# A hybrid mLSTM and S5 block on one core: conversions, attention steps and the merge put in another order

## The chip, the cores and the metric

The kernel runs on one core of a Trainium2 chip. The core has a matrix engine (PE), a vector engine (DVE), a scalar engine (ACT), a general engine (POOL) and SyncE (SP), on whose queue this kernel issues its DMA transfers. Each engine works off its own instructions in order and waits on semaphores that the others raise. The metric is the device time of one execution, in microseconds (us).

## The reference

The input is x, 1024 tokens by 1024 channels, in float32. The reference computes, for one layer:

```python
xn = rmsnorm(x, norm_pre_g)
u_a, z_a, o_a, i_a, f_a, u_b, z_b, g_pre = split(xn @ w_in)
y_a = mlstm_branch(u_a, z_a, o_a, i_a, f_a, ...) @ w_a_out
y_b = s5_branch(u_b, z_b, ...) @ w_b_out
g = sigmoid(g_pre)
merged = g[:, :1024] * y_a + g[:, 1024:] * y_b
out = x + rmsnorm(merged @ w_o, norm_post_g)
# mlstm_branch, for each of 4 heads of width 256, in 8 chunks of 128 tokens:
c = silu(causal_conv(u_a, width 4) + conv_b)
q, k, v = c @ w_q, c @ w_k, u_a @ w_v
h = chunkwise gated attention of q, k, v with a 256 x 256 state carried from chunk to chunk
h = rmsnorm(sigmoid(o_a) * h) * head_g + skip * c;  h = h * silu(z_a)
```

## The kernel before

**Precision.** Each float32 operand of a large product is kept as a pair, a high part (names ending in h: wh, xh, hlh, mh) and the rest (wl, xl, hll, ml), and `dot3` issues three matmuls for each step: high x high (L180), then the two mixed ones (L181, L182). A weight comes from DRAM as raw tile wr. `split_w` makes wh on ACT (L140) and wl = wr - wh on DVE (L142), in pieces of at most 128x1024; with `pl=True` the second and later pieces of wl are made by POOL.

**Weights in turn.** `order` lists the weights in the order of their use. `fetch` issues the DMAs of the next raw weight, `pump` converts the raw weight that has come (if none is converted and waiting) and puts off a `fetch`, and `take` hands out the converted one and, unless told not to, pumps the next.

**Units.** The program is written as units, each a group of matmuls into one PSUM bank of 512 float32 with the work on the other engines that empties it. There are three banks named pp for projections and five named pm for attention. `run` and `fill` issue a unit; `fill(n)` takes the next n from the list `fillers`. `defer` puts off a unit's second part to a later unit, and a unit's loads (its `pre`) are issued `look[0]` units ahead.

**Heads.** While head h does its attention, chunk by chunk, the projections of head h+1 fill the gaps: first eight o_units (the output gate, 24 matmuls of 128x256 each), then u and z units. In a chunk, `attn_a(h, c)` forms the scores and the scaled keys ksh and ksl, `attn_b(h, c)` uses them against v; `attn_d(h, hf)` normalises a half (L1170, DVE, tile hr), and transposes it (L1180, PE, 8 transposes). Behind chunk 7 come five `late` units in the order u2, k0, v0, u3, v1. The unit u3 is the `u_unit` with m = 1 and hf = 1: it makes hlh and hll, pumps the next weight, and does a width-4 causal convolution over its bank: a bias on ACT (tile t2k), then on DVE for each of three taps an operation on the bank (L961) and a small one on the columns kept from the half before (L964, halo). In the last head there is no next head; the fillers are units of y_a (`ya_unit`), which multiply six of the eight channel tiles' worth of head outputs by w_a_out's quarters, tile names y_t1 and y_gb, and store partial sums to the DRAM buffer pa_d.

**Merge and output.** `ya_unit(3, ...)` makes the last quarter of y_a's partial sums, `mg_unit(ct, hf)` reads ft and fpa (`mg_pre`'s loads of t1_d and pa_d), adds the remaining channel tiles with the weight called ya3, and writes mh (ACT) and ml (POOL). `wo_unit(i, t)` multiplies the merged rows of row block t (128 tokens) by quarter i of w_o, squares the bank on ACT for the norm (fjk, with the sum in sso) and multiplies it by the norm's weight on DVE (ob). The order of all of this is the order in which the Python code issues it; no scheduler moves it.

Of the kernel before, what the change touches and what calls it, by code (L numbers as in the profile page):

```python
# [10 lines left out]
F32 = mybir.dt.float32  # L11
# [3 lines left out]
ALU = mybir.AluOpType  # L15
# [21 lines left out]
def hybrid_block(ctx, tc, x, norm_pre_g, w_in, conv_w, conv_b, w_q, w_k, w_v, b_i, b_f, head_g,  # L37
# [49 lines left out]
    def defer(f, n=1):  # L87
        stage2.append([n, f])
# [854 lines left out]
    def u_unit(h, m, hf):  # L943
        o = bank()
        proj_cm(o, cur["u"], m * P, xh, xl, HS[hf])
        ct = 2 * h + m
        hi, lo = ht((P, 512), "hlh", 5, F32R), ht((P, 512), "hll", 5, F32R)
        A.activation(hi, o, AF.Copy)
        tt(lo, o, hi.bitcast(F32), ALU.subtract)
        uhl[h, m, hf] = (hi, lo)  # L950
        if m and hf:
            pump(pl=True)
        acc = ht((P, 512), "t2k", 6)
        A.activation(acc, o, AF.Identity, scale=cw[:, 3, ct:ct + 1], bias=cb[:, ct:ct + 1])
        if hf == 0:
            hl_ = ht((P, 4), "halo", 4)
            V.tensor_copy(hl_[:, 0:3], o[:, 509:512])
            halo[h, m] = hl_
        for j in (2, 1, 0):
            s = 3 - j  # L960
            V.scalar_tensor_tensor(acc[:, s:], o[:, :512 - s], cw[:, j, ct:ct + 1], acc[:, s:],  # L961
                                   op0=ALU.mult, op1=ALU.add)
            if hf == 1:
                V.scalar_tensor_tensor(acc[:, :s], halo[h, m][:, 3 - s:3], cw[:, j, ct:ct + 1],  # L964
                                       acc[:, :s], op0=ALU.mult, op1=ALU.add)
        defer(lambda: u_act(h, m, hf, acc), (3 if h < H - 1 else 2) if m and hf else 1)

    def u_act(h, m, hf, acc):
# [246 lines left out]
            SY.dma_start(yh[k][:, HS[hf]].bitcast(F32), yh_d[k * P:(k + 1) * P, HS[hf]])  # L1215
            SY.dma_start(yl[k][:, HS[hf]].bitcast(F32), yl_d[k * P:(k + 1) * P, HS[hf]])

    yaux = {}

    def ya_pre(ct, hf, pool=None):  # L1220
        rs = slice(ct * P, (ct + 1) * P)
        pool, a, b, n = (hp, "hlh", "hll", 5) if pool is None else (pool, "ft", "fpa", 7)
        t1 = pool.tile([P, 512], F32, tag=a, bufs=n, name="y_t1")
        SY.dma_start(t1, t1_d[rs, HS[hf]])
        gb = pool.tile([P, 512], F32, tag=b, bufs=n, name="y_gb")
        SY.dma_start(gb, gb_d[rs, HS[hf]])
        yaux[ct, hf] = (t1, gb)

    def ya_unit(i, m, hf):
        if m == 0 and hf == 0 and i < 3:  # L1230
            cur["ya"] = take(("ya", i), i > 0)
        ct = 2 * i + m
        rs = slice(ct * P, (ct + 1) * P)
        t1, gb = yaux.pop((ct, hf))
        o = bank()
        proj_cm(o, cur["ya"], m * P, yh, yl, HS[hf], ks=list(range(6)))
        V.scalar_tensor_tensor(t1, t1, 1.0, o, op0=ALU.add, op1=ALU.mult)
        V.scalar_tensor_tensor(gb, gb, 0.25, t1, op0=ALU.mult, op1=ALU.add)
# [30 lines left out]
    for h in range(H):  # L1269
        k1 = unit(ks[1])  # L1270
        if h < H - 1:
            us, os_, zs = proj_units(h + 1)
            ks, vs_ = kv_units(h + 1)
            late = [us[2], ks[0], vs_[0], us[3], vs_[1]]
            mix = os_ + [us[0], zs[0], us[1], zs[1], zs[2], zs[3]]
            fillers.extend(unit(f) for f in mix)
            fillers.insert(6, k1)
        else:
            late = []
            for i in range(3):  # L1280
                for hf in range(2):
                    for m in range(2):
                        fillers.append(unit(lambda i=i, m=m, hf=hf: ya_unit(i, m, hf),
                                            lambda ct=2 * i + m, hf=hf: (ct, hf) in yaux or ya_pre(ct, hf)))
            fillers.insert(3, k1)
        look[0] = 2 if h == H - 1 else 1
        load_so(h, 0)
        load_so(h, 1)
        if h == H - 1:
            for i in range(2):  # L1290
                fillers[i][0]()
                fillers[i] = (None,) + fillers[i][1:]
        ystep(4)
        if h < H - 1:
            fill()
        attn_a(h, 0)
        for c in range(NCH):
            if c == 1 or c == 6:
                load_cz(h, c // 4)
            if c == 6 and h == H - 2:  # L1300
                alloc_y(0)
            fill()
            ystep(3)
            if 1 <= c < NCH - 1:
# [12 lines left out]
            if c % 4 != 3 if h < H - 1 else c in (2, 4, 6):
                fill()
        if h == H - 1:
            fill(2)  # L1320
            attn_d(h, 1)
        for i, f in enumerate(late):
            run(unit(f))
            if i == (3 if h < H - 2 else 2):
                attn_d(h, 1)
            if i == 3 and h == H - 2:
                ya_pre(0, 0)
                alloc_y(1)
                ystep(2)
        while fillers:  # L1330
            fill()
        tick()
    cur["ya"] = take(("ya", 3))
    flush2()
    hb_.close()

# [2 lines left out]
    gpo = fp.tile([P, D], F32, name="gpo")  # L1339
    SY.dma_start(gpo, norm_post_g[0].partition_broadcast(P))  # L1340
    mh, ml = {}, {}
    maux = {}

    def mg_pre(ct, hf):
        rs = slice(ct * P, (ct + 1) * P)
        t1 = fp.tile([P, 512], F32, tag="ft", bufs=7, name="ft")
        SY.dma_start(t1, t1_d[rs, HS[hf]])
        pr = fp.tile([P, 512], F32, tag="fpa", bufs=7, name="fpa")
        SY.dma_start(pr, pa_d[rs, HS[hf]])
        maux[ct, hf] = (t1, pr)  # L1350

    def mg_unit(ct, hf):
        if ct == 0 and hf == 0:
            cur["ya3"] = take("ya3", False)
        t1, pr = maux.pop((ct, hf))
        o = bank()
        proj_cm(o, cur["ya3"], ct * P, yh, yl, HS[hf], ks=[6, 7])
        V.scalar_tensor_tensor(t1, t1, 1.0, o, op0=ALU.add, op1=ALU.mult)
# [4 lines left out]
        defer(lambda: PL.tensor_tensor(ml[ct, hf], t1, mh[ct, hf].bitcast(F32), op=ALU.subtract))  # L1363

    ob, xres = {}, {}
    sso = fp.tile([P, NCH, 4], F32, name="sso")

    def wo_unit(i, t):
        if t == 0:
            cur["wo", i] = take(("wo", i), i > 0)  # L1370
        if i == 0:
            ob[t] = main.tile([P, D], F32, tag=f"xh{t}", name=f"ob{t}")
            xres[t] = main.tile([P, D], F32, tag=f"xl{t}", name=f"xr{t}")
        if i == 1:
            SY.dma_start(xres[t], x[0, t * P:(t + 1) * P, :])
# [7 lines left out]
        A.activation(jk, o[:, :256], AF.Square, accum_out=sso[:, t, i:i + 1])
        mul(ob[t][:, cs], o[:, :256], gpo[:, cs])
        if i == 3:
            s = fp.tile([P, 1], F32, tag="fs", bufs=4, name="fs")
            V.tensor_reduce(s, sso[:, t, :], axis=mybir.AxisListType.X, op=ALU.add)
            V.tensor_scalar(s, s, 1.0 / D, 4.0 * EPS, op0=ALU.mult, op1=ALU.add)
            PL.tensor_tensor(s, s, halfm[:, 0:1], op=ALU.pow)
            finish(t, s)  # L1390

# [5 lines left out]
            store(out[0, t * P:(t + 1) * P, qs_], ob[t][:, qs_])  # L1397

    def mgf(ct, hf):
        fillers.append(unit(lambda: mg_unit(ct, hf), lambda: mg_pre(ct, hf)))  # L1400

    def yaf(m, hf):
        fillers.append(unit(lambda: ya_unit(3, m, hf), lambda: ya_pre(6 + m, hf, fp)))

    todo = deque((ct, hf) for hf in range(2) for ct in range(KT))
    for m, hf in ((0, 0), (1, 0), (0, 1), (1, 1)):
        yaf(m, hf)
        mgf(*todo.popleft())
        mgf(*todo.popleft())
    for ct, hf in todo:  # L1410
        mgf(ct, hf)
    look[0] = 3
    for i in range(3):
        fillers[i][0]()
        fillers[i] = (None,) + fillers[i][1:]
    fill(10)
    pump()
    fill(4)
    for t in range(NCH):
        run(unit(lambda: wo_unit(0, t)))  # L1420
        fill(3)
        if t == 1:
            pump()
    for i in range(1, 4):
# [32 lines left out]
```

## Time and profile before

| | |
|---|---|
| median of 3 runs | 1007.21 us (1006.0, 1007.21, 1008.55) |
| profiled execution | 1006.37 us, span 1004.3 us |
| busy PE, DVE, ACT, POOL | 976.7, 615.5, 351.1, 154.6 us |
| DMA | 148.31 MB, mean 148 GB/s |
| chain that ended last | PE 83%, DVE 10%, DMA 3% |

The span is the time from the first to the last instruction that the profiler saw; the execution's own time has some 2 us more. A row of a timeline has the start, the length, the engine, the line, the operation, output <- input, the shape, and in brackets the idle time just before it with what ended that.

### The profile page before, as it was taken

To read this page: it belongs to the slowest core of one execution; us is meant where nothing else is said; L and a number is where in the kernel's file an instruction comes from. 1 tells how busy PE (TensorE), PEld (TensorE's weight loads), DVE (VectorE), ACT (ScalarE), POOL (GpSimd) and SP (SyncE) were. 2 spreads that over 40 slices of the span, in tenths; PEclk is the share of its full clock that TensorE was granted. 3 is DMA by queue.
4 is the path that set the end of the run, shared out by engine and by line. 5 is a ranking of instruction groups with operands and counts; after the bars stand their busy time and mean duration, and the time that the engine had idled before them with its cause. 6 is when DMAs were issued, how large, how long until landed. Compare 5 with 4: busy or idle time off the path is not lost.

```text
span 1004.3 us, 15220 instructions
## 1 busy us (share of the span) xinstructions
PE 976.7 (97%) x5617; PEld 840.9 (84%) x5617; DVE 615.5 (61%) x1400; ACT 351.1 (35%) x696; POOL 154.6 (15%) x210
## 2 busy tenths in 40 slices
PE   7999999999999999999999999999999999999997
PEld 6888888788778788978988899889987888779997
DVE  4426496686952854254677477747774888675226
ACT  7322131233032531223544355435543452223311
POOL 4001000000000000012112232223221311343001
PEclk8999999999999999999999999999999999999999
DMA  7344221333056447314433354336436796783504
GB/s 253 94 153 157 90 95 36 93 111 109 17 177 187 170 156 253 107 42 126 138 121 131 95 174 131 135 86 184 132 121 215 248 318 202 271 301 118 189 1 168
DMA packets 115449, 148.31 MB, mean 148 GB/s; under 512 B 19080, under 2 KB 71472, under 8 KB 115376
## 3 DMA queue, kind: packets, MB, share of 16 engines
q1 hardware_dynamic: 115376, 147.35, 45.7%
q8 instruction: 44, 0.72, 0.3%
q14 instruction: 29, 0.24, 0.1%
HBM read 100.88 MB, written 46.43 MB: 147 GB/s over the span
## 4 chain that ended last, share of the span: by engine, by line
PE 83%; DVE 10%; DMA 3%; issue 2%; ACT 1%; SPq 0%; POOL 0%; DVEq 0%; POOLq 0%; ACTq 0%
PE pp L180 22%; PE pp L182 22%; PE pp L181 22%; PE pm L182 4%; PE pm L180 4%; PE pm L181 3%; DVE wl L142 1%; PE pm L1084 1%; DMA wr<-in_w_in_dram 1%; DVE zt L439 1%; PE pm L1007 1%; DMA xt<-in_x_dram 1%; DMA ft<-t_d 1%; PE pm L661 1%; DVE ec_r L439 1%
## 5 line engine op out<-in xcount | busy, mean ns | idle before, releaser
L180 PE MATMUL pp<-xh,wh 128*128 128x512 f32 x768 | 307.6, 401 | 3.2 <-DVE xl L276 2.4
L182 PE MATMUL pp<-xh,wl 128*128 128x512 f32 x768 | 305.0, 397 | 4.4 <-DVE wl L142 4.4
L181 PE MATMUL pp<-xl,wh 128*128 128x512 f32 x768 | 304.7, 397 | 0.0
L182 PEld LDWEIGHTS pp<-xh,wl 128*128 128x128 f32 x768 | 145.0, 189 | 41.0 <-DVE wl L142 6.2
L180 PEld LDWEIGHTS pp<-xh,wh 128*128 128x128 f32 x768 | 145.0, 189 | 39.3 <-DVE xl L276 2.7
L181 PEld LDWEIGHTS pp<-xl,wh 128*128 128x128 f32 x768 | 145.1, 189 | 32.7
L142 DVE TENSOR_TENSOR wl<-wr,wh 128x1024 fp32r<-128x1024 f32 (+2 forms) x71 | 83.4, 1211 | 46.3 <-ACT wh L140 41.7
L140 ACT ACTIVATE wh<-wr 128x1024 fp32r<-128x1024 f32 (+2 forms) x76 | 73.2, 1008 | 40.8 <-PE pm L181 30.7
L182 PE MATMUL pp<-wh,ml 128*128 128x256 f32 x256 | 72.8, 284 | 0.5 <-POOL ml L1363 0.5
L180 PE MATMUL pp<-wh,mh 128*128 128x256 f32 x256 | 72.9, 285 | 0.0
L180 PE MATMUL pp<-wh,xh 128*128 128x256 f32 (+1 forms) x256 | 72.0, 281 | 0.0
L181 PE MATMUL pp<-wl,mh 128*128 128x256 f32 x256 | 71.9, 281 | 0.0
L288 ACT ACTIVATE tg<-pp 128x512 f32<-128x512 f32 x32 | 19.1, 599 | 151.1 <-PE pp L182 75.2
L181 PE MATMUL pp<-wl,xh 128*128 128x256 f32 (+1 forms) x256 | 71.8, 280 | 0.0
L182 PE MATMUL pp<-wh,xl 128*128 128x256 f32 (+1 forms) x256 | 71.8, 280 | 0.0
L182 PEld LDWEIGHTS pp<-wh,ml 128*128 128x128 f32 x256 | 48.1, 188 | 0.7 <-POOL ml L1363 0.7
L181 PEld LDWEIGHTS pp<-wl,mh 128*128 128x128 f32 x256 | 48.6, 190 | 0.1
L180 PEld LDWEIGHTS pp<-wh,mh 128*128 128x128 f32 x256 | 48.4, 189 | 0.2 <-ACT mh L1362 0.2
L181 PEld LDWEIGHTS pp<-wl,xh 128*128 128x128 f32 x256 | 48.2, 188 | 0.2
L180 PEld LDWEIGHTS pp<-wh,xh 128*128 128x128 f32 x256 | 48.1, 188 | 0.2
L182 PEld LDWEIGHTS pp<-wh,xl 128*128 128x128 f32 x256 | 48.0, 187 | 0.0
L981 POOL TENSOR_TENSOR hll<-t2k,hlh 128x512 fp32r<-128x512 f32 x16 | 20.8, 1297 | 166.2 <-ACT hlh L980 89.4
(395 smaller groups left out, 1731.5 us busy)
## 6 DMA issues: line engine op xcount, KB each, us to landing
wr<-in_w_in_dram SPq DMA_DIRECT2D x48, 512.0 KB
t_d<-tg SPq DMA_DIRECT2D x32, 256.0 KB
xt<-in_x_dram SPq DMA_DIRECT2D x8, 512.0 KB
aux<-t_d SPq DMA_DIRECT2D x16, 256.0 KB
gb_d<-aux SPq DMA_DIRECT2D x16, 256.0 KB
so_d<-sow SPq DMA_DIRECT2D x32, 128.0 KB
sz_d<-t2k SPq DMA_DIRECT2D x16, 256.0 KB
cs_d<-t2k SPq DMA_DIRECT2D x16, 256.0 KB
```

The costliest lines, as they stand in the source:

```text
L140: A.activation(hi, raw, AF.Copy)
L142: eng.tensor_tensor(wl[:, k0:k0 + n, c0:c0 + w], raw, hi.bitcast(F32), op=ALU.subtract)
L180: PE.matmul(o, lh, rh, start=first, stop=False)
L181: PE.matmul(o, lh, rl, start=False, stop=False)
L182: PE.matmul(o, ll, rh, start=False, stop=last)
L288: A.activation(t, o, AF.Tanh, scale=0.5)
L439: V.tensor_tensor(o, a, b, op=op)
L661: PE.matmul(o[NS * b2:NS * (b2 + 1), g * P:(g + 1) * P], q["wt"][:, ri, g, NS * b2:NS * (b2 + 1)], ut[b][:, 2 * g + b2, :], start=True, st ...
L981: PL.tensor_tensor(lo, acc, hi.bitcast(F32), op=ALU.subtract)
L1007: PE.matmul(pm[:, 256 * k:256 * k + 256], wt[:, e, 256 + P * k:256 + P * k + P], wt[:, e, 0:256], start=e == 0, stop=e == 1)
L1084: PE.matmul(sc[:, :P], k_[:, m, sl], q_[:, m, sl], start=m == 0, stop=m == 1)
```

## The change

In words, part by part:

- `u_unit`: the pump stands behind the convolution instead of ahead of it.
- The heads' loop: two fillers between attn_a(h, 0) and attn_b(h, 0) instead of one, and one more or less at two other chunks to keep the count; attn_d of the second-last head stands behind u3, as in the other heads; two of the four deferred y loads of the last head's entry come later.
- Before the merge: the last quarter of w_a_out is taken without a pump, and ya3 is pumped with `pl=True`.
- `ya_unit(3, ...)`: its four results stay on chip (tiles fyt, fyg, fyp), so that for channel tiles 6 and 7 the stores to pa_d and the loads in `mg_pre` are left out; ft and fpa have 4 buffers instead of 7.
- The merge's list: ya(0,0), ya(1,0), mg(6,0), mg(7,0), mg(0,0), ya(0,1), mg(1,0), ya(1,1), and then the rest, instead of one ya and two mg in turn. With fill(6) and then fill(2) for each row block (before: 4 and 3) the pump at t = 1 stands ahead of the last two merge units (ct = 4, 5 of the second half).
- `wo_unit`: the norm's sum over the first three quarters is formed with the third; the mean's factor is in the square's scale; the last addition is POOL's.

```diff
         tt(lo, o, hi.bitcast(F32), ALU.subtract)
         uhl[h, m, hf] = (hi, lo)
-        if m and hf:
-            pump(pl=True)
         acc = ht((P, 512), "t2k", 6)
         A.activation(acc, o, AF.Identity, scale=cw[:, 3, ct:ct + 1], bias=cb[:, ct:ct + 1])
...
                 V.scalar_tensor_tensor(acc[:, :s], halo[h, m][:, 3 - s:3], cw[:, j, ct:ct + 1],
                                        acc[:, :s], op0=ALU.mult, op1=ALU.add)
+        if m and hf:
+            pump(pl=True)
         defer(lambda: u_act(h, m, hf, acc), (3 if h < H - 1 else 2) if m and hf else 1)
 
...
             SY.dma_start(yl[k][:, HS[hf]].bitcast(F32), yl_d[k * P:(k + 1) * P, HS[hf]])
 
-    yaux = {}
+    yaux, maux = {}, {}
 
     def ya_pre(ct, hf, pool=None):
         rs = slice(ct * P, (ct + 1) * P)
-        pool, a, b, n = (hp, "hlh", "hll", 5) if pool is None else (pool, "ft", "fpa", 7)
+        pool, a, b, n = (hp, "hlh", "hll", 5) if pool is None else (pool, "fyt", "fyg", 2)
         t1 = pool.tile([P, 512], F32, tag=a, bufs=n, name="y_t1")
         SY.dma_start(t1, t1_d[rs, HS[hf]])
...
         o = bank()
         proj_cm(o, cur["ya"], m * P, yh, yl, HS[hf], ks=list(range(6)))
-        V.scalar_tensor_tensor(t1, t1, 1.0, o, op0=ALU.add, op1=ALU.mult)
+        t1_ = t1
+        if i == 3:
+            t1 = fp.tile([P, 512], F32, tag="fyp", bufs=2, name="fyp")
+        V.scalar_tensor_tensor(t1, t1_, 1.0, o, op0=ALU.add, op1=ALU.mult)
         V.scalar_tensor_tensor(gb, gb, 0.25, t1, op0=ALU.mult, op1=ALU.add)
-        store(pa_d[rs, HS[hf]], gb)
+        if i < 3:
+            store(pa_d[rs, HS[hf]], gb)
+        else:
+            maux[ct, hf] = (t1_, gb)
 
     def proj_units(h):
...
                 fillers[i][0]()
                 fillers[i] = (None,) + fillers[i][1:]
-        ystep(4)
+        ystep(4 if h < H - 1 else 2)
         if h < H - 1:
             fill()
...
             if c == 6 and h == H - 2:
                 alloc_y(0)
-            fill()
+            fill(2 if c == 0 and h < H - 1 else 1)
             ystep(3)
             if 1 <= c < NCH - 1:
...
             if c == 1:
                 decay(h, 1)
-            if c % 4 != 3 if h < H - 1 else c in (2, 4, 6):
+            if c in (1, 2, 4, 5, 6) if h < H - 1 else c in (2, 4, 6):
                 fill()
         if h == H - 1:
...
         for i, f in enumerate(late):
             run(unit(f))
-            if i == (3 if h < H - 2 else 2):
+            if i == 3:
                 attn_d(h, 1)
             if i == 3 and h == H - 2:
...
             fill()
         tick()
-    cur["ya"] = take(("ya", 3))
+    cur["ya"] = take(("ya", 3), False)
+    pump(pl=True)
     flush2()
     hb_.close()
...
     SY.dma_start(gpo, norm_post_g[0].partition_broadcast(P))
     mh, ml = {}, {}
-    maux = {}
 
     def mg_pre(ct, hf):
         rs = slice(ct * P, (ct + 1) * P)
-        t1 = fp.tile([P, 512], F32, tag="ft", bufs=7, name="ft")
+        t1 = fp.tile([P, 512], F32, tag="ft", bufs=4, name="ft")
         SY.dma_start(t1, t1_d[rs, HS[hf]])
-        pr = fp.tile([P, 512], F32, tag="fpa", bufs=7, name="fpa")
+        pr = fp.tile([P, 512], F32, tag="fpa", bufs=4, name="fpa")
         SY.dma_start(pr, pa_d[rs, HS[hf]])
         maux[ct, hf] = (t1, pr)
 
     def mg_unit(ct, hf):
-        if ct == 0 and hf == 0:
+        if "ya3" not in cur:
             cur["ya3"] = take("ya3", False)
         t1, pr = maux.pop((ct, hf))
...
 
     ob, xres = {}, {}
-    sso = fp.tile([P, NCH, 4], F32, name="sso")
+    sso = fp.tile([P, NCH, 5], F32, name="sso")
 
     def wo_unit(i, t):
...
         cs = slice(256 * i, 256 * (i + 1))
         jk = fp.tile([P, 256], F32, tag="fjk", bufs=2, name="fjk")
-        A.activation(jk, o[:, :256], AF.Square, accum_out=sso[:, t, i:i + 1])
+        A.activation(jk, o[:, :256], AF.Square, scale=1.0 / 32.0, accum_out=sso[:, t, i:i + 1])
         mul(ob[t][:, cs], o[:, :256], gpo[:, cs])
+        if i == 2:
+            V.tensor_reduce(sso[:, t, 4:5], sso[:, t, 0:3], axis=mybir.AxisListType.X, op=ALU.add)
+            V.tensor_scalar(sso[:, t, 4:5], sso[:, t, 4:5], 4.0 * EPS, None, op0=ALU.add)
         if i == 3:
             s = fp.tile([P, 1], F32, tag="fs", bufs=4, name="fs")
-            V.tensor_reduce(s, sso[:, t, :], axis=mybir.AxisListType.X, op=ALU.add)
-            V.tensor_scalar(s, s, 1.0 / D, 4.0 * EPS, op0=ALU.mult, op1=ALU.add)
+            PL.tensor_tensor(s, sso[:, t, 3:4], sso[:, t, 4:5], op=ALU.add)
             PL.tensor_tensor(s, s, halfm[:, 0:1], op=ALU.pow)
             finish(t, s)
...
 
     def mgf(ct, hf):
-        fillers.append(unit(lambda: mg_unit(ct, hf), lambda: mg_pre(ct, hf)))
+        fillers.append(unit(lambda: mg_unit(ct, hf), lambda: (ct, hf) in maux or ct > 5 or mg_pre(ct, hf)))
 
     def yaf(m, hf):
         fillers.append(unit(lambda: ya_unit(3, m, hf), lambda: ya_pre(6 + m, hf, fp)))
 
-    todo = deque((ct, hf) for hf in range(2) for ct in range(KT))
-    for m, hf in ((0, 0), (1, 0), (0, 1), (1, 1)):
-        yaf(m, hf)
-        mgf(*todo.popleft())
-        mgf(*todo.popleft())
-    for ct, hf in todo:
+    yaf(0, 0)
+    yaf(1, 0)
+    mgf(6, 0)
+    mgf(7, 0)
+    mgf(0, 0)
+    yaf(0, 1)
+    mgf(1, 0)
+    yaf(1, 1)
+    n_ya = len(fillers)
+    for ct, hf in [(ct, 0) for ct in range(2, 6)] + [(6, 1), (7, 1)] + [(ct, 1) for ct in range(6)]:
         mgf(ct, hf)
     look[0] = 3
...
         fillers[i][0]()
         fillers[i] = (None,) + fillers[i][1:]
-    fill(10)
+    fill(n_ya)
     pump()
-    fill(4)
+    fill(6)
     for t in range(NCH):
         run(unit(lambda: wo_unit(0, t)))
-        fill(3)
+        fill(2)
         if t == 1:
             pump()
...
```

What the change moves, at three places. In the lists a name's number tells which tile of that name it is. First DVE at u3 of head 1, which is issued behind the attention of head 0; pp_5213 is u3's bank, wl_5243 (before) and wl_5251 (after) the next weight, which the first o_unit among the fillers of the next head reads. Before:

```order
L439 TENSOR_TENSOR hll_5239<-pp_5213,hlh_5238 128x512
L142 TENSOR_TENSOR wl_5243<-wr_5100,wh_5242 128x1024
L961 SCALAR_TENSOR_TENSOR t2k_5248<-pp_5213,par_147,t2k_5248 128x511
L964 SCALAR_TENSOR_TENSOR t2k_5248<-halo_4890,par_147,t2k_5248 128x1
L961 SCALAR_TENSOR_TENSOR t2k_5248<-pp_5213,par_147,t2k_5248 128x510
L964 SCALAR_TENSOR_TENSOR t2k_5248<-halo_4890,par_147,t2k_5248 128x2
L961 SCALAR_TENSOR_TENSOR t2k_5248<-pp_5213,par_147,t2k_5248 128x509
L964 SCALAR_TENSOR_TENSOR t2k_5248<-halo_4890,par_147,t2k_5248 128x3
L1182 SCALAR_TENSOR_TENSOR t2k_5261<-pm_5256,par_147,cz_4902 128x512
```

After:

```order
L439 TENSOR_TENSOR hll_5239<-pp_5213,hlh_5238 128x512
L959 SCALAR_TENSOR_TENSOR t2k_5242<-pp_5213,par_147,t2k_5242 128x511
L962 SCALAR_TENSOR_TENSOR t2k_5242<-halo_4890,par_147,t2k_5242 128x1
L959 SCALAR_TENSOR_TENSOR t2k_5242<-pp_5213,par_147,t2k_5242 128x510
L962 SCALAR_TENSOR_TENSOR t2k_5242<-halo_4890,par_147,t2k_5242 128x2
L959 SCALAR_TENSOR_TENSOR t2k_5242<-pp_5213,par_147,t2k_5242 128x509
L962 SCALAR_TENSOR_TENSOR t2k_5242<-halo_4890,par_147,t2k_5242 128x3
L142 TENSOR_TENSOR wl_5251<-wr_5100,wh_5250 128x1024
L1182 SCALAR_TENSOR_TENSOR t2k_5261<-pm_5256,par_147,cz_4902 128x512
```

The conversion moved behind all six operations of the convolution; ACT's bias and its two wh changed places in the same way.

Second SP's queue at the merge, around the raw weights of w_o's second quarter, wr. Before:

```order
L1347 DMA ft_8793<-t1_d_68 128x512
L1349 DMA fpa_8795<-pa_d_81 128x512
L82 DMA pa_d_81<-y_gb_8735 128x512
L124 DMA wr_8826<-in_w_o_dram 128x4x256
L124 DMA wr_8828<-in_w_o_dram 128x4x256
L1347 DMA ft_8830<-t1_d_68 128x512
L1349 DMA fpa_8832<-pa_d_81 128x512
L1347 DMA ft_8846<-t1_d_68 128x512
```

After:

```order
L1353 DMA ft_8751<-t1_d_68 128x512
L1355 DMA fpa_8753<-pa_d_81 128x512
L124 DMA wr_8784<-in_w_o_dram 128x4x256
L124 DMA wr_8786<-in_w_o_dram 128x4x256
L1353 DMA ft_8788<-t1_d_68 128x512
L1355 DMA fpa_8790<-pa_d_81 128x512
```

Before, three loads for channel tiles 2, 3 and 4 and the last store of y_a stand ahead of wr. After, ft_8788 and fpa_8790, of channel tile 5, the last merge unit ahead of the second half's tiles 6 and 7, are the first behind it, and no store stands there.

Third ACT at the beginning of the product with w_o; wh_9047 (before) and wh_9005 (after) is the high part of w_o's second quarter, and mh41 to mh71 belong to merge units of the second half. Before:

```order
L1383 ACTIVATE fjk_9005,sso_8597<-pp_8980 128x256
L1362 ACTIVATE mh51_9018<-ft_8928 128x512
L1362 ACTIVATE mh61_9030<-ft_8944 128x512
L1362 ACTIVATE mh71_9043<-ft_8961 128x512
L140 ACTIVATE wh_9047<-wr_8826 128x1024
L140 ACTIVATE wh_9047<-wr_8828 128x1024
L1383 ACTIVATE fjk_9084,sso_8597<-pp_9059 128x256
L1383 ACTIVATE fjk_9115,sso_8597<-pp_9090 128x256
```

After:

```order
L1368 ACTIVATE mh21_8989<-ft_8864 128x512
L1368 ACTIVATE mh31_9001<-ft_8912 128x512
L140 ACTIVATE wh_9005<-wr_8784 128x1024
L140 ACTIVATE wh_9005<-wr_8786 128x1024
L1389 ACTIVATE fjk_9042,sso_8597<-pp_9017 128x256
L1368 ACTIVATE mh41_9055<-ft_8928 128x512
L1368 ACTIVATE mh51_9067<-ft_8976 128x512
L1389 ACTIVATE fjk_9098,sso_8597<-pp_9073 128x256
```

Before, the conversion stands behind all merge units (mh51 to mh71 are the last), and only the squares from row block 3 on (pp_9059) follow it. Now it stands ahead of the square of row block 2 (pp_9017) and of the last two merge units (mh41, mh51).

## The prediction

> **Bound.** I read the page's first and second part, then PE's waits, then timelines around each wait.
>
> ```profile
> span 1004.3 us, 15220 instructions
> PE 976.7 (97%) x5617; PEld 840.9 (84%) x5617; DVE 615.5 (61%) x1400; ACT 351.1 (35%) x696; POOL 154.6 (15%) x210
> ...
> PEclk8999999999999999999999999999999999999999
> ```
>
> PE is busy for 97% of the span; 27.6 us are idle, and nothing else comes near. The change leaves PE's instructions as they are, so it can act only on PE's idle time, on what follows PE's last matmul, and on the clock. Which of that idle time the change touches is in the table of PE's waits (total, times, longest):
>
> ```profile
> PE pp L182 <- DVE wl L142: 4.4, 4, 1.3
> ...
> PE pm L180 <- ACT ksh L1098: 1.5, 2, 0.7
> PE pm L1180 <- DVE hr L1170: 1.5, 1, 1.5
> ...
> PE pm L180 <- issue: 0.7, 1, 0.7
> PE pm L182 <- DVE ksl L1103: 0.6, 2, 0.3
> PE pp L180 <- DVE ob L439: 0.6, 1, 0.6
> PE pp L182 <- POOL ml L1363: 0.5, 1, 0.5
> PE pm L180 <- ACT hlh L948: 0.4, 1, 0.4
> PE pp L180 <- DVE ft L1358: 0.2, 1, 0.2
> PE pm L182 <- DVE hll L439: 0.2, 1, 0.2
> ```
>
> The first row holds four waits, of which two lie at the merge (below); the others lie before the heads.
>
> **Gains.** Head beginnings: a second o_unit (24 matmuls, 2.8 us at the 0.12 us between the two PE rows quoted below) stands between attn_a and attn_b of chunk 0. That is longer than each of the waits there: 0.7 (issue), 1.5 (ksh), 0.6 (ksl); all 2.8 us go. Last head's entry: attn_d(2,1) comes one unit later, which covers the wait for hr (1.5) and, since its 8 transposes now stand between u3 and v1, those for hlh and hll (0.4, 0.2): 2.1. Merge start: two units that need ya3's weights now stand ahead of the next two. Of these waits the rows are
>
> ```profile
> 867.26 0.50 PE L182 MATMUL pp<-xh,wl 128*128 128x512 f32 x1 [0.99 <-DVE wl L142]
> 869.49 0.50 PE L182 MATMUL pp<-xh,wl 128*128 128x512 f32 x1 [1.27 <-DVE wl L142]
> ```
>
> 2.3 us go: ya3's split is asked for earlier and first needed by the fifth unit. The three waits at the merge's end, on ob, ml and ft (0.6, 0.5, 0.2), lie at places that get new waits; I take off 1.3 and price the new ones below. The rows after a wait show 0.50 for a matmul of usually 0.39: a restart costs about 0.1 to 0.2. Thirteen waits go and about ten come: 0.6 off. Stores and loads of y_a's last quarter, 4 and 8 of 256 KB, are off PE's path: nothing by themselves, since PE's waits on loads here come from their order on the queue. At the last head's entry two loads (y_t, y_gb) stand ahead of four others on SP, for PE units some 18 us later; they delay those by about what two issues take in the wr row below, 1.5 us, and I take no cost (bounds 0 and 0.5).
>
> The tail:
>
> ```profile
> 998.57 0.42 DVE L439 TENSOR_TENSOR ob<-pp,gpo 128x256 f32<-128x256 f32 x1
> 998.91 0.15 DVE L1387 TENSOR_REDUCE fs<-sso 128x1 f32<-128x4 f32 x1
> 999.09 0.15 DVE L1388 TENSOR_SCALAR fs<-fs 128x1 f32<-128x1 f32 x1
> 999.39 0.54 POOL L1389 TENSOR_TENSOR fs<-fs,halfm 128x1 f32<-128x1 f32 x1 [2.34 <-DVE fs L1388]
> ```
>
> From 998.57 to 999.39 are 0.82 us of DVE ahead of POOL's power. Afterwards POOL starts when ACT's sum is there (about when the first row starts) with a small add of its own, which at least costs what a tiny DVE operation does (0.15) and at most the power's 0.54. I take 0.4 off, nearer to the POOL row (bounds 0.82 less these, 0.3 and 0.7). The two small operations per row block that move to the third quarter cost nothing: DVE is 61% busy. Gains: 2.8 + 2.1 + 2.3 + 1.3 + 0.6 + 0.4 = 9.5.
>
> **Heads.** The last u unit of a head now converts the next weights behind its convolution. The same place before, between heads 0 and 1 (DVE, POOL, ACT, PE):
>
> ```profile
> 576.70 0.69 DVE L439 TENSOR_TENSOR hll<-pp,hlh 128x512 fp32r<-128x512 f32 x1 [1.04 <-ACT hlh L948]
> 577.64 1.22 DVE L142 TENSOR_TENSOR wl<-wr,wh 128x1024 fp32r<-128x1024 f32 x1 [0.26 <-ACT wh L140]
> 579.26 0.75 DVE L961 SCALAR_TENSOR_TENSOR t2k<-pp,par,t2k 128x511 f32<-128x511 f32 x1 [0.40 <-ACT t2k L954]
> 579.93 1.23 DVE L964 SCALAR_TENSOR_TENSOR t2k<-halo,par,t2k 128x1 f32<-128x1 f32 x1
> 581.74 0.20 DVE L964 SCALAR_TENSOR_TENSOR t2k<-halo,par,t2k 128x2 f32<-128x2 f32 x1
> ...
> 578.64 2.50 POOL L142 TENSOR_TENSOR wl<-wr,wh 128x1024 fp32r<-128x1024 f32 x1 [2.62 <-ACT wh L140]
> ...
> 576.56 2.00 ACT L140 ACTIVATE wh<-wr 128x1024 fp32r<-128x1024 f32 x2
> 578.46 0.77 ACT L954 ACTIVATE t2k<-pp,par 128x512 f32<-128x512 f32 x1
> ...
> 579.79 0.28 PE L180 MATMUL pp<-wh,xh 128*128 128x256 f32 x1
> 579.90 0.28 PE L181 MATMUL pp<-wl,xh 128*128 128x256 f32 x1
> ```
>
> The second of the PE rows is the first reader of this wl: the conversion ended at 578.86, 1.0 us early. That is 3.2 us after hll's start; call hll's start zero. Now ACT does the bias (t2k, 0.77) first, once hll is done: 0.72 to 1.45. Its two wh follow to 3.4, POOL's half runs 3.5 to 6.0. On DVE the three pairs of convolution operations run from 1.5 (pair 0.75 + 0.20, less overlap), and the last small one would start at 3.8, inside POOL's 2.50 us. What happens then, the row at 579.93 shows: 1.23 instead of 0.20, ending at 581.16, just when POOL's row ended. So it ends at 6.0, wl runs 5.95 to 7.15, and PE goes on at 7.2 instead of 3.2: a wait of 4.0. Bounds: without that clash wl runs 3.9 to 5.1, a wait of 2.0; if DVE slips its wl in ahead of POOL, POOL's half comes late, some 3.0. I take 4.0, since the row shows the clash in the very place, with the same two instructions. [...]
>
> The same stands between heads 1 and 2: 4.0. Before head 0 there is more work between:
>
> ```profile
> 472.57 0.69 DVE L439 TENSOR_TENSOR hll<-pp,hlh 128x512 fp32r<-128x512 f32 x1 [3.18 <-ACT hlh L948]
> 477.46 0.28 PE L181 MATMUL pp<-wl,xh 128*128 128x256 f32 x1
> ```
>
> Needed at 4.9, ready at 7.2: a wait of 2.3 (bound 0.2 without the clash). In the last head's entry the weights are y_a's first, 128x1024 and 128x512: ACT and POOL have half as much for the second, so wl is ready about 1.4 earlier, at 5.8. It is needed at about 4.0 (3.2 as above, plus attn_a's 0.6 and a step): 1.8 (bounds 0 and 3.2). DVE's work for attn_d(2,1) now comes there later and may delay ksh of that head: 0 to 0.8, I take 0.4. Heads together: 2.3 + 4.0 + 4.0 + 1.8 + 0.4 = 12.5.
>
> **Merge.** On SP's queue the load of ft for the last unit of the first half now stands behind the raw weights of w_o's second part, whose buffers wait for a DVE conversion. Before, the analogous load came so:
>
> ```profile
> 891.12 0.32 SPq L82 DMA_DIRECT2D pa_d<-y_gb  x1
> 892.26 1.52 SPq L124 DMA_DIRECT2D wr<-in_w_o_dram  x2
> ...
> 899.91 0.69 DVE L1358 SCALAR_TENSOR_TENSOR ft<-ft,pp 128x512 f32<-128x512 f32 x1 [2.20 <-DMA ft<-t_d]
> ```
>
> The store at 891.12 ends y_a; two DVE operations of 0.7 lie between PE's last y_a matmul and it, so PE ended at 889.7. The wr issue followed that by 2.6, and the ft operation followed the wr issue by 7.7; with its own 0.7 the bank is free 10.9 after y_a's end. After the change PE has six merge units of six 0.233 us matmuls in between, 8.4 us, before it needs that bank: 2.5, less a little for the restart, 2.4 (bounds 0, if the load slips ahead, and 4). The ml of the same unit, 0.5 late before, is then 0 to 0.8 late, 0.4.
>
> At row block t = 1 the next conversion of w_o now stands on ACT and DVE ahead of the last two merge units. Its wh overwrites a buffer that the second of these units still reads, so ACT waits for PE; behind it on ACT stands the square of wo(0,2), behind that on DVE the ob product that frees the bank for wo(0,3), which is PE's next unit. Before, all merge units were done by then:
>
> ```profile
> 913.95 2.00 ACT L140 ACTIVATE wh<-wr 128x1024 fp32r<-128x1024 f32 x2
> 915.85 0.36 ACT L1383 ACTIVATE fjk<-pp 128x256 f32<-128x256 f32 x1
> ...
> 915.03 2.98 DVE L142 TENSOR_TENSOR wl<-wr,wh 128x1024 fp32r<-128x1024 f32 x2 [1.65 <-ACT wh L140]
> 917.93 0.74 DVE L439 TENSOR_TENSOR ob<-pp,gpo 128x256 f32<-128x256 f32 x2
> ```
>
> From ACT's start to the first ob product's end (half of the last row): 917.93 + 0.37 - 913.95 = 4.35. DVE there idled until 915.03; at its own pace (1.0 until the first wh, 2 x 1.22, 0.4) 3.8. All of it is a PE wait: 3.8 (bounds 2.6, where only ACT's row counts, and 4.4). Merge: 2.4 + 0.4 + 3.8 = 6.6.
>
> **The clock.** What a stall of this size does to TensorE's clock, one place of this trace shows (columns: stretch, length, busy time per engine, granted clock, DMA share, GB/s):
>
> ```profile
> 298.04:301.45 3.41, 1.36 (x9) 0.94 (x7) 3.29 (x6) 0.60 (x1) 0.00 (x0) 1.00 0.00 0
> 301.45:304.87 3.42, 3.42 (x16) 3.42 (x17) 1.12 (x2) 0.00 (x0) 0.00 (x0) 0.50 0.41 154
> ```
>
> After a stretch of 3.41 us with PE busy for 1.36 (2.05 idle), the next ran at 0.50. A wait of 4 us leaves about 2 us idle in one such stretch wherever it falls. Half a clock for 3.42 us is 1.7 us lost; for the three waits of about 4 that is 5.1 (bounds 0 and, with the waits of 1.8 to 2.4, 10). [...]
>
> **Sum.** 1006.4 (the profiled execution, span 1004.3 and 2.1 around it; 0.8 below the median of the runs) - 9.5 + 12.5 + 6.6 + 5.1 = 1021.1.
>
> **Rivals.** (a) The waits come, the clock stays: 1016.0. For it: it takes one place only to make the clock term. Against it: that place was busy to 40% and fell all the same. (b) No clash of POOL and DVE: the heads cost 0.2 + 2.0 + 2.0 + 0.4 and y_a nothing, 4.6, and only w_o's wait touches the clock: 1006.4 - 9.5 + 4.6 + 6.6 + 1.7 = 1009.8. Against it speaks the 1.23 us row. (c) Faster: the conversions that move are all hidden, by PE reaching the first reader of wl late, being itself held by something else. Then the head's 12.5, the 3.8 and the clock's 5.1 vanish: 1006.4 - 9.5 + 2.8 = 999.7. It decides from where the moved conversions cost less than 6.7 together; the 1.0 us of slack at 578.86 against a shift of some 5 speaks against it. (d) The new waits come at half their size and cancel the gains: 1006.4 - 9.5 + 9.5, near 1006.4.
>
> **Numbers.** This kernel can be told from no change by about 0.3%, 3 us. Main case 0.52 (1017 to 1026), (a) 0.18, (b) 0.14, (c) 0.08, (d) 0.08. The first three are slower: 0.84, less a part of (b), whose value lies at the edge, 0.83; (d) and that part 0.09; (c) 0.08. The range from 1008 to 1026 leaves out (c), (d) and the main case's far end.
>
> **What would show it.** PE waits at the first o_unit behind v1 for wl (4 us twice, 2.3 once), POOL's wl row overlapping a small convolution operation of 2 us; a wait of 1.8 at y_a's first unit; 2.4 for ft at the start of w_o; 3.8 for ob at wo(0,3); granted clock 0.5 behind these; waits for hr, ksh, ksl and ya3's wl gone; POOL's power about 0.4 nearer to the last matmul. I am wrong if wl does not appear in the waits at the heads, or if the clock rows stay at 1.00.

## The result and the profile after

The changed kernel takes 1021.62 us in the median of 4 runs (1020.89 to 1028.11), the kernel before 1007.69 (4 runs, 1006.0 to 1008.55); the ratio on record is 1.0169, 95% interval 1.0144 to 1.0194. These two medians alone give 1.0138, which lies below that interval; the runs printed here do not show where the difference comes from, and both figures are clear of the noise. The forecast was 1021.1. Here are the page's first lines and PE's waits of the changed kernel, those from 0.2 us on that the prediction spoke of or should have:

```profile
span 1019.8 us, 15197 instructions
PE 981.2 (96%) x5617; PEld 845.7 (83%) x5617; DVE 615.9 (60%) x1399; ACT 351.8 (34%) x696; POOL 158.6 (16%) x219
...
PE pp L181 <- DVE wl L142: 9.4, 3, 3.7
PE pp L180 <- DVE ob L439: 3.7, 1, 3.7
PE pp L182 <- DVE wl L142: 3.3, 3, 1.2
...
PE pp L180 <- DVE ft L1364: 2.6, 2, 2.4
...
PE pp L180 <- DMA xh<-yh_d: 1.4, 1, 1.4
PE pp L181 <- DMA xl<-yl_d: 0.4, 2, 0.2
PE pm L182 <- DVE ksl L1103: 0.3, 1, 0.3
PE pm L180 <- ACT ksh L1098: 0.2, 1, 0.2
```

PE's idle time rose from 27.6 to 38.6 us (1019.8 - 981.2), and its busy time by 4.5 us with the same 5617 instructions, at a mean granted clock of 0.988 against 0.993: the clock. The waits for hr and hlh are gone, ksh and ksl shrank from 2.1 to 0.5, and of `L182 <- DVE wl` the two at the merge are gone (one of its three, 1.2 us, is new, at y_a's first unit). The wait for wl at the heads' first o_units (L181, 9.4) is new, and so are the long one for ob, the one for ft and those for xh and xl.

The head between 0 and 1, the place of the prediction's longest working: DVE, POOL, PE.

```profile
575.29 0.69 DVE L439 TENSOR_TENSOR hll<-pp,hlh 128x512 fp32r<-128x512 f32 x1 [1.05 <-ACT hlh L948]
578.29 0.21 DVE L962 SCALAR_TENSOR_TENSOR t2k<-halo,par,t2k 128x2 f32<-128x2 f32 x1
579.07 2.06 DVE L962 SCALAR_TENSOR_TENSOR t2k<-halo,par,t2k 128x3 f32<-128x3 f32 x1
581.06 1.21 DVE L142 TENSOR_TENSOR wl<-wr,wh 128x1024 fp32r<-128x1024 f32 x1
...
578.78 2.34 POOL L142 TENSOR_TENSOR wl<-wr,wh 128x1024 fp32r<-128x1024 f32 x1 [4.18 <-ACT wh L140]
...
582.33 0.58 PE L181 MATMUL pp<-wl,xh 128*128 128x256 f32 x1 [3.67 <-DVE wl L142]
```

The last small convolution operation, on three columns, took 2.06 us where its sister took 0.21, and ended at 581.13, as POOL's did (581.12). Behind it came wl, and behind that PE, which had waited 3.67 us. The stretches of 3.41 us around it (PE's busy time is the second figure, the granted clock the third from the end):

```profile
578.03:581.44 3.41, 0.63 (x6) 0.42 (x4) 3.41 (x5) 1.64 (x3) 2.46 (x4) 1.00 0.01 2
581.44:584.85 3.41, 2.52 (x12) 2.53 (x13) 3.34 (x5) 0.63 (x1) 0.45 (x1) 0.50 0.78 205
584.85:588.27 3.42, 3.42 (x18) 3.42 (x18) 1.39 (x3) 1.01 (x2) 2.57 (x2) 0.50 0.87 312
588.27:591.68 3.41, 3.41 (x31) 3.41 (x30) 1.07 (x3) 0.84 (x3) 0.00 (x0) 1.00 0.68 217
```

One wait cost two stretches at half the clock: at the full clock PE's 2.52 + 3.42 us of work there would have taken half as long, 3.0 us less (an estimate: it takes PE to be held up by nothing else). At the other head the same wait cost one stretch (690.66 to 694.07, 1.7 us), at w_o's start one (1.7), at wo(0,3) two (2.7): 9.1 us together.

At wo(0,3), ACT, DVE and PE:

```profile
923.70 2.00 ACT L140 ACTIVATE wh<-wr 128x1024 fp32r<-128x1024 f32 x2 [3.34 <-PE pp L181]
...
924.79 2.36 DVE L142 TENSOR_TENSOR wl<-wr,wh 128x1024 fp32r<-128x1024 f32 x2 [5.09 <-ACT wh L140]
927.07 0.42 DVE L439 TENSOR_TENSOR ob<-pp,gpo 128x256 f32<-128x256 f32 x1
...
927.54 0.58 PE L180 MATMUL pp<-wh,mh 128*128 128x256 f32 x1 [3.69 <-DVE ob L439]
```

ACT had waited for PE's last merge unit; then the conversion, the ob product and PE followed one upon the other. And the tail, POOL and DVE:

```profile
1014.35 0.19 POOL L1396 TENSOR_TENSOR fs<-sso 128x1 f32<-128x1 f32 x1 [2.06 <-ACT fjk L1389]
1014.62 0.54 POOL L1397 TENSOR_TENSOR fs<-fs,halfm 128x1 f32<-128x1 f32 x1
...
1015.21 1.42 DVE L1403 SCALAR_TENSOR_TENSOR ob<-ob,fs,xr 128x512 f32<-128x512 f32 x2 [0.47 <-POOL fs L1397]
```

From ACT's last square to DVE's last products it took 1.41 us (1013.80 to 1015.21), before 1.91 (998.06 to 999.97): 0.50 gained.

### The profile page after: what moved, and what is told of

Read it like the earlier page. It is cut to its first block, busy times and chain, and to the rows that moved or that the text cites. A ratio compares the mean times of both kernels' runs of the same rounds, so it can differ in the third digit from the quotient of the medians.

```text
span 1019.8 us, 15197 instructions
## 1 busy us (share of the span) xinstructions
PE 981.2 (96%) x5617; PEld 845.7 (83%) x5617; DVE 615.9 (60%) x1399; ACT 351.8 (34%) x696; POOL 158.6 (16%) x219
## 4 chain that ended last, share of the span: by engine, by line
PE 80%; DVE 9%; DMA 5%; issue 2%; ACT 1%; SPq 1%; POOL 0%; DVEq 0%; POOLq 0%; ACTq 0%
PE pp L180 22%; PE pp L181 22%; PE pp L182 22%; PE pm L182 3%; PE pm L180 3%; PE pm L181 3%; DMA xl<-yl_d 2%; PE pm L1084 1%; DVE wl L142 1%; DVE zt L439 1%; DVE t2k L962 1%; PE pm L1007 1%; DMA fpa<-pa_d 1%; DMA xt<-in_x_dram 1%; DMA ft<-t_d 1%
## 5 line engine op out<-in xcount | busy, mean ns | idle before, releaser
L182 PE MATMUL pp<-xh,wl 128*128 128x512 f32 x768 | 304.2, 396 | 3.3 <-DVE wl L142 3.3
L181 PE MATMUL pp<-xl,wh 128*128 128x512 f32 x768 | 304.1, 396 | 0.4 <-DMA xl<-yl_d 0.4
L182 PEld LDWEIGHTS pp<-xh,wl 128*128 128x128 f32 x768 | 144.4, 188 | 39.4 <-DVE wl L142 4.7
L181 PEld LDWEIGHTS pp<-xl,wh 128*128 128x128 f32 x768 | 144.6, 188 | 33.6 <-DMA xl<-yl_d 1.0
L142 DVE TENSOR_TENSOR wl<-wr,wh 128x1024 fp32r<-128x1024 f32 (+2 forms) x70 | 80.5, 1185 | 47.9 <-ACT wh L140 43.4
L181 PE MATMUL pp<-wl,xh 128*128 128x256 f32 (+1 forms) x256 | 74.0, 289 | 9.4 <-DVE wl L142 9.4
L181 PE MATMUL pp<-wl,mh 128*128 128x256 f32 x256 | 74.1, 289 | 0.0
L182 PE MATMUL pp<-wh,ml 128*128 128x256 f32 x256 | 73.5, 287 | 0.0
L182 PE MATMUL pp<-wh,xl 128*128 128x256 f32 (+1 forms) x256 | 73.5, 287 | 0.0
L181 PEld LDWEIGHTS pp<-wl,xh 128*128 128x128 f32 x256 | 50.0, 195 | 10.2 <-DVE wl L142 10.0
L182 PEld LDWEIGHTS pp<-wh,ml 128*128 128x128 f32 x256 | 50.5, 197 | 0.0
L181 PEld LDWEIGHTS pp<-wl,mh 128*128 128x128 f32 x256 | 50.0, 195 | 0.1
L182 PEld LDWEIGHTS pp<-wh,xl 128*128 128x128 f32 x256 | 49.9, 195 | 0.0
```

The costliest lines, as they stand in the source:

```text
L142: eng.tensor_tensor(wl[:, k0:k0 + n, c0:c0 + w], raw, hi.bitcast(F32), op=ALU.subtract)
L181: PE.matmul(o, lh, rl, start=False, stop=False)
L182: PE.matmul(o, ll, rh, start=False, stop=last)
```

## The experiments

Eight kernels, each run beside the kernel before. Four ran on one chip, where that took 1005.29 us in the median: the pump ahead again, both pieces of wl on DVE, the pump at t = 2 and the work for PE. The other four ran on another, 1005.68.

**The pump of u3 ahead of the convolution again.**

```diff
         uhl[h, m, hf] = (hi, lo)
+        if m and hf:
+            pump(pl=True)
...
-        if m and hf:
-            pump(pl=True)
         defer(lambda: u_act(h, m, hf, acc), (3 if h < H - 1 else 2) if m and hf else 1)
```

> The changed kernel with one part undone: the pump of the unit u3 stands ahead of the convolution again. Theory (the moved conversion is late for the first o_unit): the waits for wl at the three heads and at y_a's first unit, 2.03 + 3.67 + 3.66 + 1.18 = 10.5 us, go, and with the two of 3.7 the half clock behind them (6.83 and 3.41 us at half speed, 3.0 + 1.7 lost): 1021.6 - 15.2 = 1006.4, 1004 to 1010. Rival (PE's time there is bound by all of the work on DVE and ACT, and a wait for ksh, ksl or hr takes the place): at least half comes back as other PE waits, 1013 or more.

Measured: 1008.98 us, ratio to before 1.0038 (1.0018 to 1.0059); the span fell from 1019.8 to 1006.1. No wait for wl is left at a head, and no half clock is there. What came instead at the heads is small: PE's waits from its table,

```profile
PE pm L180 <- ACT ksh L1098: 1.1, 1, 1.1
PE pp L180 <- ACT sow L835: 0.6, 2, 0.3
...
PE pm L180 <- DVE hr L1149: 0.4, 2, 0.2
```

The theory holds: of the 15.5 us by which the changed kernel's span stands above that of before, 13.7 are gone with this one call (spans of single executions; the medians beside each kernel leave 3.7 of 13.9). The largest wait left that the kernel before does not have is the one at wo(0,3), 3.7 us as it was, with its half clock; in the merge ft has 2.0 us and ml 1.1.

**The part alone.** In the kernel before:

```diff
         uhl[h, m, hf] = (hi, lo)
-        if m and hf:
-            pump(pl=True)
...
+        if m and hf:
+            pump(pl=True)
         defer(lambda: u_act(h, m, hf, acc), (3 if h < H - 1 else 2) if m and hf else 1)
```

> The kernel before with one part of the change alone: the pump of u3 behind the convolution. Theory (this part by itself makes the loss at the heads): waits for wl of 2.0, 3.7 and 3.7 us appear at the three heads' first o_units, with half clock behind the two longer ones (1.7 to 3.0 us each), 12.8 to 15.4 slower than the kernel before beside it, ratio 1.013 to 1.015. Rival (the waits need the rest of the change, as the second o_unit that stands earlier): under 6 us slower, ratio under 1.006.

Measured: 1017.04 us against 1005.68, ratio 1.0109 (1.0087 to 1.0132), span 1013.3. The rival falls, but the forecast of 1.013 to 1.015 was too high too. The waits came as expected:

```profile
PE pp L181 <- DVE wl L142: 9.4, 3, 3.7
PE pp L182 <- DVE wl L142: 5.6, 5, 1.3
```

But its table has no wait for ksh, ksl or "issue" any more, 2.8 us in the kernel before: while PE stands at the first o_unit, ACT and DVE have time to get done what attn_b needs soon after. That is the likely reason; what the table shows is that a wait put ahead of others has swallowed them. These 2.8 us go without the second o_unit, then, and in the changed kernel, where the same wait for wl stands, that unit had nothing to hide.

**Both pieces of wl on DVE.**

```diff
         if m and hf:
-            pump(pl=True)
+            pump()
```

> The changed kernel, pump of u3 at its new place, but both pieces of wl on DVE and none on POOL. Theory (the last small convolution operation waits out POOL's instruction): it takes 0.2 instead of 2.06 us, the first wl ends 1.9 earlier, the waits at the heads are 0.2, 1.8 and 1.8 instead of 2.03, 3.67 and 3.66, and no half clock follows them: 1011, 1008 to 1014. Rival (DVE has simply too much to do there, with or without POOL): with 1.2 us more on DVE the waits are as long as now or longer, 3.7 and more.

Measured: 1011.65 us in one run, span 1009.9. DVE and PE at the same head:

```profile
577.65 0.21 DVE L962 SCALAR_TENSOR_TENSOR t2k<-halo,par,t2k 128x3 f32<-128x3 f32 x1
577.78 2.36 DVE L142 TENSOR_TENSOR wl<-wr,wh 128x1024 fp32r<-128x1024 f32 x2
...
579.05 0.38 PE L181 MATMUL pp<-wl,xh 128*128 128x256 f32 x1 [1.81 <-DVE wl L142]
```

With POOL out of the way the small operation takes 0.21 us, and PE waits 1.81 us (both later heads; at the first one none over 0.15): DVE does more and PE waits less. So of the 3.67 us some 1.85 are the clash with POOL, and 1.8 the order alone. Not every DVE operation beside POOL's was held up: in the kernel before the convolution operation that reads the PSUM bank kept its 0.75 us (579.26) while POOL's 2.50 us ran (from 578.64). Why the small operation waits and this one does not was not shown. One expectation missed: at one of the two heads a half clock did follow,

```profile
576.80:580.21 3.41, 1.60 (x13) 1.40 (x13) 3.41 (x7) 1.45 (x3) 0.00 (x0) 1.00 0.06 7
580.21:583.63 3.42, 3.42 (x19) 3.42 (x17) 3.35 (x6) 1.23 (x3) 1.36 (x1) 0.50 0.98 283
```

because the whole wait fell into one stretch and left 1.60 us of work in it; at the other head the same 1.81 us (682.17 to 683.98) lay across two, and the clock stayed at 1.00.

**Pump at t = 2.**

```diff
-        if t == 1:
+        if t == 2:
             pump()
```

> The changed kernel with the pump of w_o's second quarter at t = 2, behind the last merge unit. Theory (ACT's wh waits for PE while PE waits for the bank behind it): the 3.69 us wait for ob at wo(0,3) goes, and the half clock behind it, 2.7 us: 1015.2, 1013 to 1018. Rival (the conversion is then late for the second quarter, or the bank is late for another reason): the wait moves to wo(0,4) or to wo(1,0) and the time stays at 1020 to 1022.

Measured: 1013.58 us, ratio to before 1.0073 (1.0047 to 1.0099). The wait for ob and the half clock there are gone, and neither wo(0,4) nor wo(1,0) waits. The kernel before is here 2.4 us faster than beside the changed kernel; less these the theory's 1015.2 is 1012.8, and 1013.58 is close to it. The profiled execution also has no half clock at w_o's start, which the theory did not count on, and one behind the 2.03 us wait at the first head, where the changed kernel had none.

**Work for PE in the wait.**

```diff
     def wo_unit(i, t):
...
+        if i == 0 and t == 3:
+            d = mbank()
+            for _ in range(13):
+                PE.matmul(d, cur["wo", 0][0][:, 0, 0:P], mh[0, 0], start=True, stop=True)
         o = bank()
```

> The changed kernel with 13 matmuls of 128x512 added on PE in the 3.69 us wait ahead of wo(0,3), into a bank that nothing reads; nothing else changes. They take 13 x 0.233 = 3.0 us of the wait. Theory (the clock falls when PE is busy for less than some 1.4 of a 3.41 us stretch): the granted clock stays at 1.00 around that wait, and the 2.7 us lost behind it come back: 1019 with about 0.6 us of the wait left. Rival (the half clock has another cause than PE's idle share, or the matmuls add their own time): half clock behind the wait as before, 1021.6 or up to 1024.6.

Measured: 1019.46 us in one run. PE's timeline, and the two stretches that hold the wait:

```profile
923.93 3.20 PE L1387 MATMUL pm<-mh,wh 128*128 128x512 f32 x13
927.79 0.39 PE L180 MATMUL pp<-wh,mh 128*128 128x256 f32 x1 [0.66 <-DVE ob L439]
...
923.15:926.56 3.41, 3.41 (x17) 2.73 (x16) 1.52 (x2) 2.37 (x4) 0.00 (x0) 1.00 0.00 0
926.56:929.98 3.41, 2.75 (x21) 2.32 (x20) 3.35 (x6) 0.63 (x1) 0.12 (x1) 1.00 0.69 217
```

The same place in the changed kernel, without the added work:

```profile
922.77:926.18 3.41, 1.07 (x5) 0.55 (x3) 1.39 (x2) 2.36 (x4) 0.00 (x0) 1.00 0.00 0
926.18:929.59 3.41, 2.05 (x9) 2.05 (x10) 3.34 (x6) 0.63 (x1) 0.00 (x0) 0.50 0.60 189
```

The granted clock stays at 1.00 around a wait that without the added work cost two stretches. ACT, DVE and the ob product behind which PE waits take as long as they did (3.79 us from ACT's start to the product's end, both times); only PE was kept busy. That here it was PE's idle share behind which the clock fell (busy for 1.07 us of the first stretch without the added work, for 3.41 with it) is thereby shown, not only seen. The whole time is a single run's, not taken beside the changed kernel, and cannot tell 2.7 us; the rows can.

**The y loads together.**

```diff
-        ystep(4 if h < H - 1 else 2)
+        ystep(4)
```

> The changed kernel with the four y loads of the last head's entry issued together again, ahead of y_t and y_gb. Theory (the 1.4 and 0.4 us waits for xh and xl at y_a's second unit come from two loads put behind two others on SP's queue): these waits go and no other wait near 800 to 815 us takes their place, 1.5 to 2.2 us off: span 1018, or less where a half clock is missed. Rival (the loads are late because the bytes ahead of them take their time, in whatever order): a wait of 1 us or more stays there, for xh or for y_t's operations.

Measured: 1021.23 us in one run, span 1019.5. The waits for xh are gone and 0.2 for xl is left, so they came from the order on SP's queue. The time of this one run did not follow. From its table of PE's waits:

```profile
PE pp L180 <- DVE ft L1364: 2.1, 2, 1.3
...
PE pp L182 <- POOL ml L1369: 1.1, 1, 1.1
...
PE pp L181 <- DMA xl<-yl_d: 0.2, 1, 0.2
```

Of the 1.5 us gained, 0.6 went to the merge (ft and ml 3.2 instead of 2.6), and eight stretches ran at half the clock instead of seven. Whether these came from the change or from where the stretches fell was not tried.

**Four repairs.** The pump of u3 ahead of the convolution, the pump at t = 2 and the y loads together, as above, and the loads of channel tile 5 ahead of w_o's second raw weight:

```diff
     fill(n_ya)
+    fillers[3][0]()
+    fillers[3] = (None,) + fillers[3][1:]
     pump()
```

> The changed kernel with four repairs: pump of u3 ahead of the convolution, pump of w_o's second quarter at t = 2, the y loads together, and the loads of the merge unit of channel tile 5 issued ahead of w_o's second raw weight. Theory (the rest of the change is a gain, head beginnings 2.8 and 1.0 of restarts and order, merge start 2.3, merge end 0 to 1.3, end 0.5): waits left at the last head's entry (ksh, about 1.4) and in the merge (ft or ml, 1 to 2): 5 to 8 us under the kernel before beside it, ratio 0.992 to 0.995. Rival (the stores and buffers of the last quarter cost what the order gains): within 2 us of before.

Measured: 999.96 us against 1005.68, ratio 0.9940 (0.9921 to 0.9959): faster than both kernels. Its page and PE's remaining waits:

```profile
span 997.3 us, 15202 instructions
PE 974.2 (98%) x5617; PEld 838.7 (84%) x5617; DVE 615.6 (62%) x1399; ACT 351.4 (35%) x696; POOL 160.6 (16%) x219
...
PE pp L182 <- POOL ml L1369: 1.3, 2, 1.1
PE pm L180 <- ACT ksh L1098: 1.1, 1, 1.1
```

PE idles for 23.1 us, before for 27.6. So the rest of the change is a gain, as the list of gains said, though of 5.7 us in the medians and not of 9.5; it was buried under the moves that the four repairs take back. The fourth of these, for ft at w_o's start, was not tried alone. (The three pairs of loads that stand ahead of these raw weights in the kernel before belong, by the order of its units, to channel tiles 6 and 7 of the first half and 0 of the second; 2, 3 and 4 are those of the changed kernel.)

**More buffers.** The kernel with the four repairs and

```diff
-        ... else (pool, "fyt", "fyg", 2)
+        ... else (pool, "fyt", "fyg", 3)
...
-            t1 = fp.tile([P, 512], F32, tag="fyp", bufs=2, name="fyp")
+            t1 = fp.tile([P, 512], F32, tag="fyp", bufs=1, name="fyp")
```

> The same with 3 instead of 2 buffers for fyt and fyg and one for fyp. Theory (y_t's loads wait for POOL's ml of the first two merge units, and DVE waits for these loads, so merge waits of 0.7 to 1.3 us come from the two buffers): 1 to 2 us faster than the kernel with the four repairs. Rival (the waits come from the loads of ft and from DVE's and POOL's own pace): equal within 0.5 us.

Measured: 1000.1 us, ratio 0.9941 (0.9919 to 0.9962), the same as with 2. The waits that are left (ml 1.3, ft 0.2) are the same, so the two buffers do not make them.

## Why the prediction was right, and where it was not

The direction and the mechanisms held, and the sum too, in part by luck (below); the terms, as measured in the changed kernel's profile:

| term | forecast, us | measured, us |
|---|---|---|
| wl before head 0, between 0 and 1, between 1 and 2 | 2.3, 4.0, 4.0 | 2.03, 3.67, 3.66 |
| wl at y_a's first unit | 1.8 | 1.18 |
| ksh and ksl at the last head | 0.4 | 0.55 |
| ft at w_o's start, then ml | 2.4, 0.4 | 2.43 and 0.18 at a unit ahead of it, 0 |
| ob at wo(0,3) | 3.8 | 3.69 |
| loads of xh, xl at y_a's second unit | 0 | 1.7 |
| tail | -0.4 | -0.50 |
| half clock behind the waits | 5.1 | 9.1 |
| half clock elsewhere | 0 | -3.3 |

The measured terms come to 24.4 us; less the 8.5 us of PE waits that stood here before, 15.9 are left, and the span grew by 15.5. The rest, 0.4, may be restarts. The parts fit less well than the whole: PE's idle time grew by 11.0 us where the terms give 10.1, and its busy time by 4.5 where the half clock gives 9.1 - 3.3 = 5.8, so the price of the half clock is rather an upper estimate.

*The clash.* The step from one row (1.23 instead of 0.20 us) to a small operation that starts at 3.8 and ends with POOL's at 6.0, behind hll's start, held to 0.2 us (3.78 and 5.84), and the kernel with both pieces on DVE shows that it is POOL. The three waits are each shorter by 0.3, about half of it because POOL's piece took 2.34, not 2.50.

*The clock.* Rival (a) is out: the granted clock fell to 0.50 behind each of the four new waits of 2.43 to 3.69 us. The price of a wait was mis-sized: one stretch, 1.7 us, for each wait of 4 us, where two of the four events took two stretches, and ft's 2.43 us had one that was left in the bounds. In the other direction, the kernel before's profile had three stretches at half clock early on (two from 14.73, one from 301.45), the changed kernel's only one (from 14.83), though the code there is the same: 4.8 less 1.5, 3.3 us that do not come from the change. (The kernel with the y loads together, which has the change, shows the same three stretches as the kernel before.) Without them the profiled execution would have stood near 1025. That the median came out at the forecast is in part luck: these two errors stand against each other.

*The gains.* The 2.8 us for ksh, ksl and "issue" were right as rows that go (0.5 is left), but wrong as something the second o_unit does here: the kernel with the pump alone shows that the new wait ahead of them removes them too. In the kernel with the four repairs, with no wait for wl ahead of them, they stay away too, but smaller waits come at the same heads (sow 0.6, hr 0.4, ksl 0.3), so about half of the 2.8 us is a gain. In the same way the 0.55 us for ksh and ksl at the last head stand behind a wait for wl; with the pump ahead again they are 1.4, above the bound of 0.8.

*The loads.* "I take no cost (bounds 0 and 0.5)" was too narrow: the next loads on SP came 1.7 us late for PE. The bounds should have had the row's 1.5 us as their upper end, since PE's slack there had not been read from a row. For ft, 2.43 us in one row is this execution's: the five other kernels that leave that order as it is have 1.3 to 1.7 there, 0.3 to 1.0 at a unit ahead of it and, for ml, 0.8 to 1.1, together 2.7 to 3.4. The size held; how it is shared out between these rows is not fixed.

*Rivals (b), (c) and (d).* The head waits without the clash, priced at 0.2, 2.0 and 2.0, are what the experiment without POOL shows (0, 1.81, 1.81): the price was right and the condition was not met. (c) needed the first reader of wl to come late; it came 3.4 us after hll's start, before the change 3.2. (d) asked for waits of half their size; they came at nine tenths.

## What to carry to other kernels

On an engine that works off its instructions in the order of the code, as DVE and ACT do in the rows above, a step that only one distant reader needs looks free to move behind others; count instead from the moment where its first reader stands, and read that reader's slack from a row before and what stands between from the order (here 1.0 us of slack against a shift of 5). If a conversion must wait for the last reader of the buffer that it overwrites, nothing that frees the next bank may be queued behind it (3.69 us at wo(0,3)). Where one engine is busy for 97% of the span, price a wait on it with its clock: here 19.1 us of waits at the heads, at the loads and in the merge cost 28 with the half clock behind them, and the same work in another order made the kernel 0.6% faster instead of 1.4 to 1.7% slower.

## What the runs showed of the hardware

In the traces of the kernel before and of the changed one the granted clock is 1.00 or 0.50, and it changes only at times that lie whole numbers of 3.413 us apart (in the changed kernel 581.44, 690.66, 905.70 and 926.18 are such times). Taken stretch by stretch, from 4.49 and 4.59 us on, both traces show the same. At full clock PE was busy for 1.39 us or less in nine stretches (before 1.39, 1.36 and, at the end, 0.20; after 1.14, 0.63, 0.43, 0.98, 1.07 and, at the end, 0), and the stretch behind each of them ran at half the clock. All others at full clock, busy for 1.65 us or more, were followed by full clock, as these two, one of the kernel before and one of the changed kernel:

```profile
4.49:7.90 3.41, 1.65 (x15) 1.42 (x14) 0.75 (x1) 3.00 (x5) 1.47 (x4) 1.00 0.94 376
...
475.63:479.04 3.41, 1.85 (x16) 1.85 (x17) 2.11 (x3) 1.27 (x5) 0.58 (x7) 1.00 0.53 148
```

With both pieces of wl on DVE a stretch busy for 1.60 us was followed by half the clock. So in these rows the two kinds part between 1.60 and 1.65 of 3.41 us (PE's ends are modelled, so the last hundredths are not to be trusted). For the way back, in the traces before and after, a slow stretch that was itself busy for 2.05, 2.52 or 2.71 us was followed by a second slow one, one with 2.92 or all of it by a fast one. Those of 2.71 and 2.92 lie near the program's start, before and after:

```profile
14.73:18.14 3.41, 2.71 (x6) 2.15 (x7) 3.27 (x5) 3.41 (x6) 2.39 (x1) 0.50 1.02 405
18.14:21.56 3.42, 3.42 (x9) 2.64 (x8) 2.77 (x7) 3.42 (x7) 1.12 (x3) 0.50 0.90 290
...
14.83:18.25 3.42, 2.92 (x7) 2.35 (x8) 3.29 (x6) 3.42 (x7) 2.39 (x1) 0.50 1.02 407
18.25:21.66 3.41, 3.41 (x17) 2.73 (x16) 2.77 (x6) 3.41 (x7) 1.34 (x3) 1.00 0.89 296
```

The same wait of 3.67 us therefore cost one stretch or two, one of 1.81 (both pieces of wl on DVE) none or one, by where it fell, and one of 2.03 in the changed kernel none: for the 3.67 us, in the changed kernel two and one at its two heads, in the one with the y loads together one and two. The spread of the unchanged kernel's runs goes with the same clock: on one chip the fastest, 1001.77 us, had a mean granted clock of 0.997 and the slowest, 1009.18, one of 0.990, and 0.007 of 1004 us are 7.0 of these 7.4. That only the place of the stretches makes this difference was not tried.
